# Token sums of the down parts made where each pair is turned, token scales inside the next group, and one early weight chunk split by halves

## The chip, the cores and the metric

The kernel runs on one core of a Trainium2 chip. The metric is the device time of one execution in microseconds (us), the median of several runs. Before the change it is 1868.39 us (three runs, 1868.15 to 1868.74).

## The reference

One layer of a decoder trunk for 256 tokens of width 2048, all in float32. Two token mixers run side by side (a gated recurrent block and stick-breaking attention); their merged output goes through `w_o` and is added to the residual `x`. Then come a SwiGLU feed-forward network and a gated per-layer embedding. The change touches the work from `w_o` on, and the first weights of the kernel:

```python
h = rmsnorm(x, g_mix[i])
proj = h @ w_in[i]                    # starts the kernel: its gate columns come first
...                                   # two mixers
x = x + mix @ w_o[i]

h = rmsnorm(x, g_ffn[i])
gu = h @ w_ffn_gu[i]                  # 2048 -> 2 x 5632
g, u = jnp.split(gu, 2, axis=-1)
x = x + (jax.nn.silu(g) * u) @ w_ffn_down[i]       # 5632 -> 2048

ple_gate = jax.nn.sigmoid(rmsnorm(x, g_ple[i]) @ w_ple_gate[i])
x = x + ple_gate * (p[i] @ w_ple_proj[i])
```

`rmsnorm(x, g)` is `x * rsqrt(mean(x*x) + eps) * g`. The factor `rsqrt(...)` is one number for each token; the kernel multiplies it in after the product ("token scale"), so the product can start before it is known.

## The kernel before

**Products.** Every float32 value is split into a high part `hi` (a rounded copy in the type fp32r) and a low part `lo` (the value less `hi`); a product is three matmuls: `hi*hi`, `hi*lo` of the weights and `lo*hi` of the activations. In function `prod` these are lines 638, 639 and 640: 638 and 639 multiply the high activations by the weights' `whi` and `wlo`, and 640 the low activations by `whi`. The tokens stand on the partitions of the result, 128 tokens by 512 columns for each matmul.

**Weight stream.** The weights come as chunks of 128 rows by 1024 columns in a fixed order. A chunk is loaded by a DMA issued on SP (SyncE), and split by ScalarE (ACT; line 366, `whi`) and then VectorE (DVE; line 367, `wlo`). There are five buffers of each. In the first group the first two k tiles are cut into chunks of 512 columns, so that chunk number 4 is k tile 2, the first of 1024 columns.

**Sums instead of products.** In most groups some k tiles are computed by a Strassen-like scheme of seven products instead of eight. It needs sums of weights and sums of activations. The sums of weights ("11", "T1", "T2", "21", ... and `("S", i, p)`) are made from raw tiles `Q` by DVE adds of 512 or 1024 columns (line 291, function `summed`) and by DMAs that add on landing (line 329, issued on POOL); then they are split like any chunk. The sums of activations are made by `half_sums`: four DVE operations of 128x128, one ACT copy of 512 columns, and one DVE subtraction of 512 columns. They are needed only for the k tiles that take part.

**Groups.** `group` runs the matmuls of one group of output columns over all its slots (a slot is a k tile or a sum). The order from `w_o` on is: wo (2 groups), gu 0 to 3 (each gives 512 feed-forward columns of gate and up), down part dn0 (2 groups), gu 4 to 7, dn1, gu 8 to 10, dn2, and the two groups pg of the per-layer gate. At the end of a group its four PSUM banks are added to the saved tiles by DVE (`tt(c, q, c, ALU.add)`, "ps adds", `H<-ps,H`). Two lists hold work that is put off into the next group: `todo` (for gu the gating, `gated`: a Silu on ACT and a `scalar_tensor_tensor` on DVE at line 449, both with the token scale `rs1`) and `pend` (the turnings: PE transposes of a pair of 128-column blocks, lines 1169 and 1230, after which the pair is split into `hi` and `lo` as the activations of a later product). In each group `TURNED_AT` says at which slots a turning is taken from `pend`.

**The sums of a down part.** The 16, 16 and 12 k tiles of dn0, dn1 and dn2 are pairs of what gu made. Of three, three and two of these pairs the activation sums are wanted. Before the change `parts_sums` makes them late, in the last gu group ahead of the down part (gu 3, 7 and 10), at slots 16, 18 and 20: a DVE add of 512 columns rebuilds the value from `hi` and `lo`, and `half_sums` follows.

**Token scales.** `token_scales` adds up eight partial sums of squares (two small DVE adds) and computes the inverse root by a logarithm and an exponential on ACT. It is called between groups: `rs1` between wo and gu 0, `rs2` between dn2 and pg 0.

**What sets the order.** The engines run their instructions in the order of five lists that a scheduler makes ahead of time from the program. `behind_splits` and `issue_after` tell it not to place an instruction ahead of a given one (the latest split of weights, or a matmul).

Of the kernel before, what the change touches and what calls it, by code (L numbers as in the profile page):

```python
# [8 lines left out]
F32 = mybir.dt.float32  # L9
# [6 lines left out]
D = 2048  # L16
# [28 lines left out]
W_BUFS = 4  # L45
RAW_AHEAD = 12.0
SUMS_AHEAD = 2
TURNED_AT = {True: (5, 7, 9, 11), False: (9, 11, 13, 15)}
NEG = -1e30


# [8 lines left out]
def is_sum(x):  # L60

    return isinstance(x, str) or isinstance(x, tuple) and x[0] == "S"
# [180 lines left out]

DMA_ORDER, DMA_UPTO = dma_order()
HALVES = (1, 3)


class Stream:
# [99 lines left out]
    def split_to(self, n):  # L348
        n = min(n, len(CHUNKS))
        while self.n_split < n:  # L350
            self.sum_to(self.n_split + 1)
            j = self.n_split
            i, a, b = CHUNKS[j]
            mode = PLAN[i][0][3] if PLAN[i][0][0] == "tok" else 0
            if is_sum(mode):
                t, c = self.sums.pop(j)
            else:
                t, c = self.raw.pop(j)[0], P * (b - a)
            o = 512 * (j in HALVES)
            if not o:  # L360
                hi = self.hi = self.phl.tile([P, 1024], F32R, tag="whi", name=f"whi_{j}")
                lo = self.lo = self.phl.tile([P, 1024], F32R, tag="wlo", name=f"wlo_{j}")
            else:
                hi, lo = self.hi, self.lo
            h, l = hi[:, o:o + c], lo[:, o:o + c]
            self.hi_ins = self.nc.scalar.activation(h, t[:, :c], AF.Copy)  # L366
            self.lo_ins = self.nc.vector.tensor_tensor(l, t[:, :c], h.bitcast(F32), ALU.subtract)  # L367
            res = self.parts.setdefault(i, [])
            for x in range(c // P):
                s = slice(o + x * P, o + (x + 1) * P)  # L370
                res.append((hi[:, s], lo[:, s], hi, lo, o + x * P))
            self.n_split += 1
            g = lambda m: (*PLAN[i][0][1:3], m)
            if mode == "T2":
                self.joins(self.raw[g("R")], 0, g("21"), 0)
            elif isinstance(mode, tuple) and mode[:2] == ("S", 2):
                self.joins(self.raw[g(("Y", mode[2]))], 512, g(("S", 1, mode[2])), 512)
# [41 lines left out]
def tile_hybrid_block(ctx: ExitStack, tc: tile.TileContext, xT: bass.AP, x: bass.AP, pT: bass.AP,  # L419
# [25 lines left out]
    def tt(o, a, b, op):  # L445
        nc.vector.tensor_tensor(o, a, b, op)  # L446
# [255 lines left out]
    def group(at, pairs, sums, after=None, also=()):  # L702
# [6 lines left out]
        name, g = at  # L709
        slots = [x for n, y, _, _, _, sl in HEAD + TAIL if (n, y) == at for x in sl  # L710
                 if isinstance(x, int) or is_sum(x)]
        seq = [(n, q, 0, 512) for n, x in enumerate(slots) for q in products(x, pairs_of(name)[:2])]
        if at == LAST_GROUP:
            k = len(slots) - 4
# [11 lines left out]
        for i, (n, (b, y, p, c), e0, e1) in enumerate(seq):  # L726
            if n not in got:
                if n in also:
                    also[n]()
                if n and todo:  # L730
                    todo.pop(0)()
                elif n in TURNED_AT[slots[2] == 6 and slots[8] == "22"] and pend:
                    with tc.issue_after(mm_.ins):
                        pend.pop(0)()
                got[n] = S_.take(("tok", name, g, slots[n]))
# [419 lines left out]

    def token_scales(i, r):
        v = ssq[i]
        tt(v[:, :4], v[:, :4], v[:, 4:], ALU.add)
        tt(v[:, :2], v[:, :2], v[:, 2:4], ALU.add)
        rsqrt_mean(r, v[:, :2], D)  # L1160

    def turned(p):

# [27 lines left out]
    for g in range(2):  # L1191
# [8 lines left out]
            squares(0, t, b)  # L1200
        for p in range(4 * g, 4 * g + 4):
            pend.append(next_h(hg, hsum, p, PC_GF))
    token_scales(0, rs1)


    acts, asum = {}, {}
    behind = {3: 0, 7: 1, 10: 2}

    def gu(g):
        also = {}  # L1210
        if g in behind:
            also = {16 + 2 * i: (lambda p: lambda: parts_sums(acts, asum, p))(p)
                    for i, p in enumerate(pairs_of(f"dn{behind[g]}"))}
        c11, c21, c12, c22 = whole(("gu", g), hg, hsum, also)
        def gated(c, s_, t):
            def run():
                actv(s_, s_, AF.Silu, scale=rs1[:, t:t + 1])
                stt(c, c, rs1[:, t:t + 1], s_, ALU.mult, ALU.mult)
            return run

        todo.extend([gated(c12, c11, 0), gated(c22, c21, 1)])

        def turn(f):
            def run():
                ps = psum()
                for e in range(2):
                    for t, a in enumerate((c12, c22)):
                        c = (2 * f + e) * P
                        o = e * 256 + t * P
                        nc.tensor.transpose(ps[:, o:o + P], a[:, c:c + P], ident)  # L1230
                acts[2 * g + f] = split(ps, "A")
            return run

        pend.extend(turn(f) for f in range(2))
# [14 lines left out]
    for name, g, _, _, _, _ in TAIL:  # L1249
        if name == "gu":  # L1250
            gu(g)
        elif name[:2] == "dn":
            down(int(name[2]), g)
    token_scales(1, rs2)
    pts = [split(pt, "X")]


# [14 lines left out]
        return run  # L1272

    for g in range(2):
        qs_, t_ = group(("pg", g), h3, sum3, also={len(FIRST3) - 4: embedded(g)})
        for n, (q, c) in enumerate(zip(qs_, ("11", "T3", "T2", "T1"))):
            t, b, op = n % 2, 2 * g + n // 2, ALU.add
            c, ps, o = t_[c], pp.pop(0), tl("T")
# [76 lines left out]
```

## Time and profile before

| | us |
|---|---|
| median of three runs | 1868.39 (1868.15 to 1868.74) |
| the profiled execution, its own time | 1867.5 |
| its span in the trace | 1865.5 |
| TensorE matmuls busy in it | 1848.0 (99%) |
| VectorE busy | 1504.6 (81%) |
| ScalarE busy | 1250.0 (67%) |
| GpSimd busy | 115.6 (6%) |

The profiled execution is 0.9 us below the median, and 2.0 us of its time lie outside the span. The mean granted clock of TensorE was 0.999 of full speed. Where groups begin and end in the span: wo to gu 0 at 1059 us, gu 3 to dn0 at 1228, gu 7 to dn1 at 1481, dn2 to pg 0 at 1760.

In the timeline a row has the start in us from the span's beginning, the duration in us, engine, line, operation, the tiles written and read with their shapes, the count of like instructions joined in the row, and in brackets the idle time of the engine just before, with what ended it. PE is TensorE. A wide matmul with 512 columns is followed by the next one after 0.227 us while nothing is waited for, though each row shows 0.39 us, since matmuls overlap. So the time that PE loses at a place is the distance of two starts less 0.227 us; it is up to 0.16 us more than the idle time in brackets. The page's names leave the numbers of buffers out.

### The profile page before, as it was taken

What the parts mean: (1) busy time and instruction counts of PE and PEld (TensorE: products, weight loads), DVE (VectorE), ACT (ScalarE), POOL (GpSimd) and SP (SyncE); (2) the same over time, 40 slices, a digit from 0 to 9 for tenths busy, and PEclk for the clock granted to TensorE, in tenths of its full rate; (3) what the DMA queues carried; (4) which work ended last, traced back from release to release, by engine and by line L of the source; (5) the groups of instructions that cost most, each with busy time, mean ns of one, the idle gap of its engine ahead of it and who ended that gap; (6) DMA issues with size and microseconds to landing.
All of it is one profiled execution on the core that took longest, in us unless ns stands there. A gap on an engine that the chain in (4) does not pass through costs nothing.

```text
span 1865.5 us, 24702 instructions
## 1 busy us (share of the span) xinstructions
PE 1848.0 (99%) x8885; PEld 1551.7 (83%) x8885; DVE 1504.6 (81%) x1896; ACT 1250.0 (67%) x1670; POOL 115.6 (6%) x140
## 2 busy tenths in 40 slices
PE   9999999999999999999999999999999999999998
PEld 7899889888888888888888788878888788888787
DVE  7688887677887576667799888898788988889886
ACT  6587888775566576677666766665566665666774
POOL 0000000000010000000000011100111001110100
PEclk9999999999999999999999999999999999999999
DMA  8556556677786654556788688877888788887774
GB/s 285 182 176 186 191 188 198 205 226 247 249 242 190 190 167 152 165 169 218 229 241 259 211 255 240 250 228 246 260 255 254 219 233 249 250 254 231 205 236 141
DMA packets 121082, 409.11 MB, mean 219 GB/s; under 512 B 13568, under 2 KB 14208, under 8 KB 120960
## 3 DMA queue, kind: packets, MB, share of 16 engines
q1 hardware_dynamic: 101808, 359.82, 55.7%
q0 software_dynamic: 19008, 47.72, 15.5%
q8 instruction: 69, 1.13, 0.2%
q14 instruction: 53, 0.43, 0.1%
q10 hardware_dynamic: 144, 0.01, 0.0%
HBM read 405.40 MB, written 2.10 MB: 218 GB/s over the span
## 4 chain that ended last, share of the span: by engine, by line
PE 94%; DVE 3%; ACT 1%; issue 1%; DMA 0%; SPq 0%; ACTq 0%; DVEq 0%
PE ps L640 25%; PE ps L639 25%; PE ps L638 25%; PE ps L568 9%; PE ps L572 5%; PE ps L552 1%; PE ps L551 1%; PE ps L550 1%; DVE wlo L367 1%; DVE H L446 1%; ACT whi L366 1%; PE ps L1230 1%; DVE Q L291 0%; PE ps L997 0%; DMA w<-in_w_dram 0%
## 5 line engine op out<-in xcount | busy, mean ns | idle before, releaser
L639 PE MATMUL ps<-wlo,Q 128*128 128x512 f32 x2185 | 851.8, 390 | 4.9 <-DVE wlo L367 4.9
L640 PE MATMUL ps<-whi,Q 128*128 128x512 f32 x2185 | 848.7, 389 | 0.0
L638 PE MATMUL ps<-whi,Q 128*128 128x512 f32 x2185 | 774.6, 391 | 5.0 <-ACT whi L366 5.0
L367 DVE TENSOR_TENSOR wlo<-w,whi 128x1024 fp32r<-128x1024 f32 (+2 forms) x497 | 599.6, 1212 | 213.6 <-ACT whi L366 208.7
L366 ACT ACTIVATE whi<-w 128x1024 fp32r<-128x1024 f32 (+2 forms) x497 | 518.7, 1049 | 258.3 <-PE ps L640 200.5
L638 PEld LDWEIGHTS ps<-whi,Q 128*128 128x128 f32 x2185 | 409.1, 188 | 92.8 <-ACT whi L366 10.2
L639 PEld LDWEIGHTS ps<-wlo,Q 128*128 128x128 f32 x2185 | 410.4, 188 | 89.5 <-DVE wlo L367 6.1
L366 ACT ACTIVATE whi<-Q 128x1024 fp32r<-128x1024 f32 (+1 forms) x339 | 339.2, 1006 | 214.0 <-PE ps L640 188.6
L640 PEld LDWEIGHTS ps<-whi,Q 128*128 128x128 f32 x2185 | 410.2, 188 | 84.8 <-DVE Q L446 0.2
L367 DVE TENSOR_TENSOR wlo<-Q,whi 128x1024 fp32r<-128x1024 f32 (+1 forms) x339 | 390.5, 1159 | 67.4 <-ACT whi L366 65.4
L329 POOL DMA_DIRECT2D Q<-in_w_dram x132 | 113.1, 864 | 1701.5 <-DVE Q L291 507.9
L568 PE MATMUL ps<-Q,whi 128*128 128x512 f32 x704 | 170.7, 392 | 0.0
L568 PEld LDWEIGHTS ps<-Q,whi 128*128 128x128 f32 x704 | 128.7, 188 | 24.5
L291 DVE TENSOR_TENSOR Q<-Q,Q 128x512 f32<-128x512 f32 (+1 forms) x132 | 115.7, 890 | 8.6 <-DMA Q<-in_w_dram 8.3
L446 DVE TENSOR_TENSOR H<-H,H 128x512 f32<-128x512 f32 (+1 forms) x208 | 117.0, 574 | 0.9 <-ACT H L452 0.5
L452 ACT ACTIVATE H<-ps 128x512 f32<-128x512 f32 (+1 forms) x163 | 84.6, 534 | 47.2 <-PE ps L640 35.8
L446 DVE TENSOR_TENSOR H<-ps,H 128x512 f32<-128x512 f32 (+1 forms) x154 | 88.7, 606 | 17.6 <-PE ps L640 12.2
L572 PEld LDWEIGHTS ps<-Q,wlo 128*128 128x128 f32 x704 | 90.4, 191 | 3.5
L572 PE MATMUL ps<-Q,wlo 128*128 128x256 f32 x704 | 91.5, 283 | 0.0
L452 ACT ACT_TABLE_LOAD x53 | 68.0, 1283 | 1.7 <-DVE Q L446 0.7
L452 ACT ACTIVATE Q<-H 128x512 fp32r<-128x512 f32 x61 | 37.5, 626 | 40.1 <-DVE H L446 39.7
L446 DVE TENSOR_TENSOR Q<-H,Q 128x512 fp32r<-128x512 f32 (+1 forms) x69 | 47.3, 688 | 1.0 <-ACT Q L452 0.7
(122 smaller groups left out, 905.2 us busy)
## 6 DMA issues: line engine op xcount, KB each, us to landing
w<-in_w_dram SPq DMA_DIRECT2D x473, 512.0 KB, 4.2
Q<-in_w_dram SPq DMA_DIRECT2D x182, 512.0 KB, 5.9
Q<-in_w_dram POOLq DMA_DIRECT2D x50, 512.0 KB, 6.3
Q<-in_w_dram POOLq DMA_DIRECT2D x82, 256.0 KB, 4.9
w<-in_w_dram SPq DMA_DIRECT2D x16, 448.0 KB, 3.3
H<-in_x_dram SPq DMA_DIRECT2D x8, 256.0 KB, 7.3
H<-in_xT_dram SPq DMA_DIRECT2D x7, 256.0 KB, 5.6
out_dram<-H SPq DMA_DIRECT2D x7, 256.0 KB, 2.8
```

Of the source, the lines that this page charges most:

```text
L291: add = lambda o, a, b: self.nc.vector.tensor_tensor(o, a, b, ALU.add)
L329: self.nc.gpsimd.dma_start(t[:, c:], src[:, a:a + 1024 - c], accum_op=ALU.add)
L366: self.hi_ins = self.nc.scalar.activation(h, t[:, :c], AF.Copy)
L367: self.lo_ins = self.nc.vector.tensor_tensor(l, t[:, :c], h.bitcast(F32), ALU.subtract)
L446: nc.vector.tensor_tensor(o, a, b, op)
L452: nc.scalar.activation(o, i, f, **kw)
L550: nc.tensor.matmul(o, wt[0], xh, start=start, stop=False)
L568: nc.tensor.matmul(pss[e], wt[0], rhs(xs, k), start=(k == 0), stop=(k == n - 1))
L572: nc.tensor.matmul(pss[e][:, :256], wt[1], rhs(xs, k)[:, :256], start=False, stop=False)
L638: nc.tensor.matmul(ps, x[0], wh, start=start, stop=False, skip_group_check=goes_on)
L639: nc.tensor.matmul(ps, x[0], wl, start=False, stop=False, skip_group_check=goes_on)
L640: return nc.tensor.matmul(ps, x[1], wh, start=False, stop=stop, skip_group_check=goes_on)
```

## The change

1. Chunk 4 alone is split as two halves of 512 columns (`SPLIT_BY_HALVES`): two ACT copies and two DVE subtractions in place of one each.
2. The activation sums of the down parts' pairs are made where the pair is turned, in the next gu group: pairs 0 and 1 in gu 1, pair 2 in gu 2, 8 and 9 in gu 5, 10 in gu 6, 16 and 17 in gu 9. For these the turned PSUM bank is copied by ACT into an SBUF tile `h`, and the split and `half_sums` read `h`. The DVE add of `parts_sums` falls away (eight times).
3. `token_scales` stands behind the latest splits, and runs at slot 10 of gu 0 (`rs1`) and of pg 0 (`rs2`).
4. In the two groups of dn2, the turnings are taken at slots 6, 8, 10, 12 (before: 9, 11, 13, 15).

The diff (line numbers behind the change are 4 to 7 higher: 366 and 367 become 370 and 371, 291 becomes 292, 446, 449 and 452 become 450, 453 and 456):

```diff
-TURNED_AT = {True: (5, 7, 9, 11), False: (9, 11, 13, 15)}
+TURNED_AT = {"first": (5, 7, 9, 11), "twelve": (6, 8, 10, 12), "even": (9, 11, 13, 15)}
...
+SPLIT_BY_HALVES = (4,)
...
-            self.hi_ins = self.nc.scalar.activation(h, t[:, :c], AF.Copy)
-            self.lo_ins = self.nc.vector.tensor_tensor(l, t[:, :c], h.bitcast(F32), ALU.subtract)
+            w = 512 if j in SPLIT_BY_HALVES else c
+            for e in range(0, c, w):
+                q = slice(e, e + w)
+                self.hi_ins = self.nc.scalar.activation(h[:, q], t[:, q], AF.Copy)
+                self.lo_ins = self.nc.vector.tensor_tensor(l[:, q], t[:, q], h[:, q].bitcast(F32), ALU.subtract)
...
+        turned_at = TURNED_AT["twelve" if len(slots) == len(TWELVE) else
+                              "first" if slots[2] == 6 and slots[8] == "22" else "even"]
...
-                elif n in TURNED_AT[slots[2] == 6 and slots[8] == "22"] and pend:
+                elif n in turned_at and pend:
...
-        tt(v[:, :4], v[:, :4], v[:, 4:], ALU.add)
-        tt(v[:, :2], v[:, :2], v[:, 2:4], ALU.add)
-        rsqrt_mean(r, v[:, :2], D)
+        with behind_splits():
+            tt(v[:, :4], v[:, :4], v[:, 4:], ALU.add)
+            tt(v[:, :2], v[:, :2], v[:, 2:4], ALU.add)
+            rsqrt_mean(r, v[:, :2], D)
...
-    token_scales(0, rs1)
...
-    behind = {3: 0, 7: 1, 10: 2}
+    summed = [p for q in range(3) for p in pairs_of(f"dn{q}")]
...
-        also = {}
-        if g in behind:
-            also = {16 + 2 * i: (lambda p: lambda: parts_sums(acts, asum, p))(p)
-                    for i, p in enumerate(pairs_of(f"dn{behind[g]}"))}
+        also = {10: lambda: token_scales(0, rs1)} if g == 0 else {}
...
-                acts[2 * g + f] = split(ps, "A")
+                p = 2 * g + f
+                if p in summed:
+                    h = tl("T")
+                    actv(h, ps, AF.Copy)
+                    acts[p] = split(h, "A")
+                    asum[p] = half_sums(h)
+                else:
+                    acts[p] = split(ps, "A")
...
-    token_scales(1, rs2)
...
-        qs_, t_ = group(("pg", g), h3, sum3, also={len(FIRST3) - 4: embedded(g)})
+        qs_, t_ = group(("pg", g), h3, sum3, also={len(FIRST3) - 4: embedded(g)} | (
+            {} if g else {10: lambda: token_scales(1, rs2)}))
```

How the order of instructions moves, at three places. In the rows `whi_516` and `wlo_516` are the two parts of chunk 516; `w32`, `Q` are raw weights, `H` working tiles, `ps` PSUM banks; in `Q_738<-H_737` a number names one tile, and the numbers of tiles differ a little between the two kernels.

VectorE around the start of dn0 (chunk 513 is its first, "11", 514 is `("S", 1, 2)`, 515 the k tile 6, 516 is "T1", 517 is `("S", 2, 2)`, 518 the k tile 7), before:

```order
L446 TENSOR_TENSOR Q_733_11115<-H_732_11110,Q_733_11115 128x512
L446 TENSOR_TENSOR H_716_10880<-ps_712_10846,H_716_10880 128x512
L446 TENSOR_TENSOR H_730_11088<-ps_713_10860,H_730_11088 128x512
L291 TENSOR_TENSOR Q_725_11054<-Q_725_11054,Q_734_11118 128x1024
L446 TENSOR_TENSOR H_722_10988<-ps_714_10864,H_722_10988 128x512
L446 TENSOR_TENSOR H_719_10937<-ps_715_10868,H_719_10937 128x512
L446 TENSOR_TENSOR Q_738_11145<-H_737_11140,Q_738_11145 128x512
L291 TENSOR_TENSOR Q_740_11174<-Q_729_11076,Q_735_11129 128x512
L446 TENSOR_TENSOR H_557_8918<-H_557_8918,H_743_11229 128x512
L449 SCALAR_TENSOR_TENSOR H_722_10988<-H_722_10988,rs1_8916,H_716_10880 128x512
L449 SCALAR_TENSOR_TENSOR H_719_10937<-H_719_10937,rs1_8916,H_730_11088 128x512
L367 TENSOR_TENSOR wlo_516_11185<-Q_725_11054,whi_516_11184 128x1024
```

and with the change:

```order
L292 TENSOR_TENSOR Q_734_11086<-Q_734_11086,Q_737_11130 128x1024
L371 TENSOR_TENSOR wlo_515_11173<-w32_515_11084,whi_515_11172 128x1024
L450 TENSOR_TENSOR H_725_10912<-ps_721_10878,H_725_10912 128x512
L450 TENSOR_TENSOR H_736_11110<-ps_722_10892,H_736_11110 128x512
L371 TENSOR_TENSOR wlo_516_11187<-Q_734_11086,whi_516_11186 128x1024
L450 TENSOR_TENSOR H_731_11020<-ps_723_10896,H_731_11020 128x512
L450 TENSOR_TENSOR H_728_10969<-ps_724_10900,H_728_10969 128x512
L371 TENSOR_TENSOR wlo_517_11208<-Q_740_11176,whi_517_11207 128x1024
L292 TENSOR_TENSOR Q_734_11086<-Q_734_11086,Q_742_11220 128x1024
L453 SCALAR_TENSOR_TENSOR H_731_11020<-H_731_11020,rs1_8918,H_725_10912 128x512
L453 SCALAR_TENSOR_TENSOR H_728_10969<-H_728_10969,rs1_8918,H_736_11110 128x512
L371 TENSOR_TENSOR wlo_518_11225<-w32_518_11139,whi_518_11224 128x1024
```

The three L446 rows that make sums of pairs (`Q_733`, `H_737`, `Q_738`) are gone from here; two of the four ps adds and the two gating rows (L449, now L453) stand behind the splits of chunks 516 and 517, where they stood ahead of 516.

ScalarE around the start of gu 0 (chunks 427, 428, 429, 430 are `("S", 2, 2)`, the k tile 7, "T2" and "21" of gu 0), before:

```order
L366 ACTIVATE whi_427_9737<-Q_628_9682 128x1024
L366 ACTIVATE whi_428_9749<-w32_428_9654 128x1024
L452 ACT_TABLE_LOAD
L452 ACTIVATE rs1_8916<-ssq0_8914,eps_t_103 128x2
L452 ACT_TABLE_LOAD
L452 ACTIVATE rs1_8916<-rs1_8916 128x2
L452 ACTIVATE H_643_9802<-ps_642_9784 128x512
L452 ACTIVATE Q_645_9812<-ps_644_9807,prm_sb_76 128x256
L366 ACTIVATE whi_429_9764<-Q_613_9521 128x1024
L366 ACTIVATE whi_430_9785<-Q_630_9700 128x1024
```

and with the change:

```order
L370 ACTIVATE whi_427_9735<-Q_628_9684 128x1024
L370 ACTIVATE whi_428_9747<-w32_428_9656 128x1024
L456 ACTIVATE H_643_9800<-ps_642_9782 128x512
L456 ACTIVATE Q_645_9810<-ps_644_9805,prm_sb_76 128x256
L370 ACTIVATE whi_429_9762<-Q_613_9523 128x1024
L370 ACTIVATE whi_430_9783<-Q_630_9702 128x1024
```

The two table loads and the two small activations that make `rs1` no longer stand between `whi_428` and `whi_429`. They stand behind chunk 439 now, ten slots on:

```order
L370 ACTIVATE whi_439_9951<-w32_439_9831 128x1024
L456 ACT_TABLE_LOAD
L456 ACTIVATE rs1_8918<-ssq0_8916,eps_t_103 128x2
L370 ACTIVATE whi_440_9958<-w32_440_9885 128x1024
L456 ACT_TABLE_LOAD
L456 ACTIVATE rs1_8918<-rs1_8918 128x2
```

ScalarE around the start of pg 0 (chunks 793 to 797 are its "T1", `("S", 2, 2)`, k tile 7, "T2" and "21"), before:

```order
L366 ACTIVATE whi_793_15685<-Q_1025_15498 128x1024
L452 ACTIVATE Q_1047_15676<-ps_1046_15671,prm_sb_76 128x256
L366 ACTIVATE whi_794_15721<-Q_1045_15655 128x1024
L366 ACTIVATE whi_795_15735<-w32_795_15638 128x1024
L452 ACT_TABLE_LOAD
L452 ACTIVATE rs2_8917<-ssq1_8915,eps_t_103 128x2
L452 ACT_TABLE_LOAD
L452 ACTIVATE rs2_8917<-rs2_8917 128x2
L366 ACTIVATE whi_796_15750<-Q_1025_15498 128x1024
L366 ACTIVATE whi_797_15771<-Q_1049_15683 128x1024
```

and with the change:

```order
L370 ACTIVATE whi_793_15687<-Q_1035_15538 128x1024
L370 ACTIVATE whi_794_15719<-Q_1047_15667 128x1024
L370 ACTIVATE whi_795_15733<-w32_795_15650 128x1024
L370 ACTIVATE whi_796_15748<-Q_1035_15538 128x1024
L370 ACTIVATE whi_797_15769<-Q_1049_15685 128x1024
```

Here too the four instructions of `rs2` and a part of the turnings (`Q_1054`, `Q_1047`) are gone from between the splits.

## The prediction

> **What bounds the kernel now.** I read the page first: the span, the busy times, the shares of the chain that ended last, and then the waits of TensorE (columns: us in all, times, longest).
>
> ```profile
> span 1865.5 us, 24702 instructions
> PE 1848.0 (99%) x8885; PEld 1551.7 (83%) x8885; DVE 1504.6 (81%) x1896; ACT 1250.0 (67%) x1670; POOL 115.6 (6%) x140
> PE 94%; DVE 3%; ACT 1%; issue 1%; DMA 0%; SPq 0%; ACTq 0%; DVEq 0%
> ...
> PE ps L638 <- ACT whi L366: 5.0, 10, 1.0
> PE ps L639 <- DVE wlo L367: 4.9, 3, 2.1
> ```
>
> TensorE bounds it, and the change leaves its work as it is. Only what PE waits can be won: ten waits for `whi` and three for `wlo`, 9.9 us of idle time, and a little more in lost spacing, since a wait costs the distance of two starts less 0.227 us. So I went to the timeline at each of these waits. They stand at four places, and the change touches each. I take them in order of time.
>
> **A. The start.** Chunk 4 is the first of 1024 columns. PE (rows 3 and 4) waits for its `wlo`.
>
> ```profile
> 10.73 1.06 ACT L366 ACTIVATE whi<-w 128x1024 fp32r<-128x1024 f32 x1 [0.35 <-DMA w<-in_w_dram]
> 11.82 2.52 DVE L367 TENSOR_TENSOR wlo<-w,whi 128x1024 fp32r<-128x1024 f32 x2 [0.90 <-ACT whi L366]
> 11.90 0.44 PE L638 MATMUL ps<-whi,Q 128*128 128x512 f32 x1
> 13.11 0.50 PE L639 MATMUL ps<-wlo,Q 128*128 128x512 f32 x1 [0.76 <-DVE wlo L367]
> ...
> 8.78 0.63 ACT L366 ACTIVATE whi<-w 128x512 fp32r<-128x512 f32 x1 [1.96 <-DMA w<-in_w_dram]
> 9.44 0.69 DVE L367 TENSOR_TENSOR wlo<-w,whi 128x512 fp32r<-128x512 f32 x1 [1.78 <-ACT whi L366]
> ```
>
> The loss is 13.11 − 11.90 − 0.23 = 0.98. With halves (0.63 and 0.69 from the last two rows), the first `whi` half ends at 10.73 + 0.63 = 11.36 and its `wlo` at about 11.39 + 0.69 = 12.08; PE asks for them at 11.90 and 12.13. The second half is wanted six matmuls after 11.90, at 13.27; it is ready by about 12.7. Two halves take 2 × 0.69 = 1.38 where one piece takes 1.22 to 1.26, so chunk 5 is split about 0.1 later, 14.35 where PE now asks at 14.6. Everything behind is asked for 1.0 earlier. **Term: −1.0**, bounds −1.1 (0.98 and the 0.1 of broken spacing behind) and −0.6 (if the DMA were late by 0.4 again, as the bracket of the first row shows it was 0.35).
>
> The Trainium skill (VectorE: DVE Perf Modes, section on the TRN2 errata) speaks against such halving: an instruction that reads SBUF pays a fixed cost each time, about 150 cycles, which an estimate at 0.96 GHz makes 0.16 us. The rows agree (1.38 against 1.22), and by that rule alone chunk 4 would cost 0.16 more; the wait it removes is six times that.
>
> **B. wo to gu 0.** ACT makes the token scale here, and PE waits for the two splits behind it.
>
> ```profile
> 1066.39 1.28 ACT L452 ACT_TABLE_LOAD   x1
> 1069.40 0.58 ACT L452 ACTIVATE H<-ps 128x512 f32<-128x512 f32 x1
> 1069.88 0.46 ACT L452 ACTIVATE Q<-ps,prm_sb 128x256 fp32r<-128x256 f32 x1
> 1070.23 2.95 ACT L366 ACTIVATE whi<-Q 128x1024 fp32r<-128x1024 f32 x3
> ...
> 1070.43 0.39 PE L640 MATMUL ps<-whi,Q 128*128 128x512 f32 x1
> 1071.35 0.51 PE L638 MATMUL ps<-whi,Q 128*128 128x512 f32 x1 [0.52 <-ACT whi L366]
> 1072.29 0.50 PE L638 MATMUL ps<-whi,Q 128*128 128x512 f32 x1 [0.44 <-ACT whi L366]
> ```
>
> ACT spends 1066.39 to 1069.40, 3.0 us, on the block that moves. Without it the two copies from PSUM run when PE has ended them, 1068.05 to 1068.6 and 1068.95 to 1069.4 (the transposes end at about 1068.98, so this second one cannot go earlier). The three `whi` then start at 1069.3 instead of 1070.23, 0.93 earlier. The first (0.98 apart, 2.95 for three) ends at 1070.35, before PE asks at 1070.66: the first loss, 1071.35 − 1070.43 − 0.23 = 0.69, goes. The second ends at 1071.3 and PE asks at about 1070.85: 0.5 of the second loss (0.72) stays. **Term: −1.1** with 0.2 of broken spacing. Bounds: −0.6 (only the first wait), −1.6 (both and the spacing).
>
> The block itself lands ten slots on, where the splits of weights have 6 to 8 us of lead (from the end of each split's row to the start of the matmul that uses it first), against 3.0 of ACT's time. It is needed by the gating, in gu 1.
>
> The Trainium skill (ScalarE: Activation LUTs, section What ACT_TABLE_LOAD costs) gives 1.28 us for the load and 1.38 for a drain. The load agrees; the drain is not seen, as the two loads and two activations take 3.0 and not 5.3 us. By the page's price B would be the same, since the copies then wait for PE, and the moved block would still fit its cover.
>
> **C. gu 3 to dn0, and gu 7 to dn1.** This is the largest. Rows of DVE, then of PE at the two places, then of ACT:
>
> ```profile
> 1228.79 0.29 DVE L446 TENSOR_TENSOR H<-H,H 128x128 f32<-128x128 f32 x1
> 1228.99 0.69 DVE L446 TENSOR_TENSOR Q<-H,Q 128x512 fp32r<-128x512 f32 x1
> 1229.59 1.28 DVE L446 TENSOR_TENSOR H<-ps,H 128x512 f32<-128x512 f32 x2
> 1230.79 1.22 DVE L291 TENSOR_TENSOR Q<-Q,Q 128x1024 f32<-128x1024 f32 x1
> 1231.92 1.29 DVE L446 TENSOR_TENSOR H<-ps,H 128x512 f32<-128x512 f32 x2
> 1233.12 0.69 DVE L446 TENSOR_TENSOR Q<-H,Q 128x512 fp32r<-128x512 f32 x1
> ...
> 1234.92 1.42 DVE L449 SCALAR_TENSOR_TENSOR H<-H,rs,H 128x512 f32<-128x512 f32 x2
> 1236.24 1.23 DVE L367 TENSOR_TENSOR wlo<-Q,whi 128x1024 fp32r<-128x1024 f32 x1
> ...
> 1235.07 0.39 PE L638 MATMUL ps<-whi,Q 128*128 128x512 f32 x1
> 1237.53 0.50 PE L639 MATMUL ps<-wlo,Q 128*128 128x512 f32 x1 [2.07 <-DVE wlo L367]
> 1239.28 0.73 PE L638 MATMUL ps<-whi,Q 128*128 128x512 f32 x2 [0.31 <-ACT whi L366]
> ...
> 1491.07 0.50 PE L639 MATMUL ps<-wlo,Q 128*128 128x512 f32 x1 [2.07 <-DVE wlo L367]
> ...
> 1233.04 1.05 ACT L366 ACTIVATE whi<-Q 128x1024 fp32r<-128x1024 f32 x1
> 1238.17 1.06 ACT L366 ACTIVATE whi<-Q 128x1024 fp32r<-128x1024 f32 x1 [4.07 <-DVE Q L291]
> ```
>
> PE asks for `wlo` of chunk 516 ("T1") at 1235.30; DVE, dense since 1228.8, starts it at 1236.24. The loss is 1237.53 − 1235.07 − 0.23 = 2.23 there, and 1.2 in the splits and spacing that are late behind it: 3.4. The same at dn1. Two things change in DVE's order, shown with the change: 0.2 + 0.6 + 0.6 = 1.4 of half sums leave, and `wlo` 516 comes right behind two ps adds. A ps add cannot start before the last products of gu 3, about 1228.8. From there: two adds of 0.60 to 1230.1, `wlo` 516 (1.14) to 1231.2, against 1235.3 wanted; two adds and `wlo` 517 to 1233.6, wanted at 1237.8; a weight sum (1.13) and the gating (1.32) to 1236.1, then `wlo` 518 to 1237.2, wanted at 1238.9. The least room is about 1 us at chunk 521, which the order puts earlier on PE. So the whole loss goes, twice: **term −6.9**; bounds −5.0 (2.5 each, if the late splits behind are late still) and −7.0.
>
> **D. dn2 to pg 0.** PE's two waits, ACT ahead of the second, and a row of busy times by stretch.
>
> ```profile
> 1767.79 0.50 PE L638 MATMUL ps<-whi,Q 128*128 128x512 f32 x1 [1.04 <-ACT whi L366]
> 1772.81 0.50 PE L638 MATMUL ps<-whi,Q 128*128 128x512 f32 x1 [0.90 <-ACT whi L366]
> ...
> 1768.71 1.28 ACT L452 ACT_TABLE_LOAD   x1
> 1771.72 2.94 ACT L366 ACTIVATE whi<-Q 128x1024 fp32r<-128x1024 f32 x3
> 1746.00:1770.00 24.00, 22.93 (x105) 18.04 (x104) 24.00 (x43) 19.61 (x34) 1.83 (x3) 1.00 0.65 202
> ```
>
> The last row (columns: stretch, its length, then busy time of PE, PEld, DVE, ACT, POOL) shows DVE without an idle moment for 24 us. Turning pairs three slots earlier moves some of its work ahead of 1746, where 1.7 us were idle, and no more. Following the new order by the same durations, the sum for "T1" comes at 1763.8, `whi` 793 by 1765.0 (no wait), `whi` 794 not before 1767.1, where PE asks at 1766.15: 0.95 stays of 1.7 (the 1.20 of this wait with spacing and a smaller one before). The table block (1768.71 to 1771.7) goes, and with it the loss of 1.06. **Term −1.85**, bounds −1.0 (the block alone) and −2.6.
>
> **What the moved work costs.** Each pair gives the gu group where it is turned one ACT copy of the bank and one of sums (0.58 + 0.63, less what a copy from PSUM took more than one from SBUF, about 1.0), and on DVE four small operations (0.2 each) and 0.6, 1.4. Two pairs are 2.8 of DVE and 2.0 of ACT. Gu 1 from slot 9 on:
>
> ```profile
> 1118.00:1144.00 26.00, 26.00 (x120) 21.53 (x119) 19.42 (x21) 17.30 (x21) 1.73 (x2) 1.00 0.81 270
> ...
> DVE wlo L367 <- ACT whi L366: 6.4, 8, 1.8
> 1386.90 0.69 DVE L367 TENSOR_TENSOR wlo<-Q,whi 128x512 fp32r<-128x512 f32 x1 [1.35 <-ACT whi L366]
> ```
>
> DVE is busy 19.4 of 26 us and waits eight times for ACT, 6.4 in all, and ACT in turn for PE to free a buffer; gu 5 shows the same waits (last row). The splits there are 4.5 to 5.8 us ahead of PE, counted the same way, and the work comes one pair at a time, two slots apart. I take **0**. Without the cover a pair costs 1.4 + 1.0 (bounds 0 to 2.4; 0 to 19 for eight). A gain is excluded, since PE loses nothing in those groups.
>
> The sum: −1.0 − 1.1 − 6.9 − 1.85 = −10.8. The profiled execution took 1867.5, so 1856.7; the median of the runs is 0.9 above it, so **1857.6**.
>
> **Rivals.** (1) *Only the half sums' own time is won at C*: the new place of `wlo` 516 is of no use because a late DMA or a late sum holds its `whi`. For it: ACT stood idle 4.07 before 1238.17, for a sum that DVE made late (the last row at C). Against: `whi` 516 began at 1233.04 (the row above that) and was done before PE asked, and the order has the sum for it earlier still. Then C is about 1.9 each, 3.8: 1860.7. Chance 0.10. (2) *ACT and DVE stay dense at B and D*, where ps adds and turnings give the pace, so that nothing comes of these: −7.9, 1860.5; with a table load in the way of one split besides, about 1862. For it: DVE's 24.00 of 24. Chance 0.12. (3) *Slower: the half sums in gu 1, 2, 5, 6 and 9 take the lead of the splits away*. If their 19 us fell on a path with no room, it would be 1857.6 + 19.2 = 1876.8, a loss; it decides once the lead of 4.5 us is eaten and DVE has no idle time between slots, that is, if the new operations wait for one another (DVE to ACT to DVE) with the queue of splits standing behind them. For it: engines run strictly in order, and the chain is three engine changes long. Against: the rows above. Half of it would give 1867. Chance 0.04 of slower, 0.06 for the half that leaves no difference. That the change does not do what it says is excluded by the order rows.
>
> **How the numbers follow.** My forecast has 0.68. The range holds the forecast's own bounds (terms −0.6 − 0.6 − 5.0 − 1.0 = −7.2 to −12.3, so 1856.1 to 1861.2) and rivals 1 and 2: 1855.0 to 1862.5, leaving out 0.1 to 0.2. A difference of 0.2% (3.7 us) is about what can be told from none, so faster needs a time below 1864.7. All of the forecast and rivals 1 and 2 are there: 0.68 + 0.10 + 0.12 = 0.90, less 0.02 for mishaps; the same 0.07; slower 0.05.
>
> **What would show it.** Right: no wait of PE longer than 0.6 us at the starts of dn0 and dn1, with `wlo` of "T1" over 3 us ahead; 0.98 gone at 11.9; at gu 0 one short wait left for the "21" chunk; at pg 0 one of about 1 us for `("S", 2, 2)` and none for "T2"; PE in gu 1, 2, 5, 6 and 9 without idle time. Wrong: new waits for `wlo` in these gu groups, or a 2 us wait at dn0 that names a `whi`.

## The result, and the profile after

The changed kernel takes 1856.93 us (median of four runs, 1856.49 to 1858.07) beside 1868.27 us for the kernel before. The ratio is 0.9940, with a 95% interval of 0.9923 to 0.9957. The predicted time was 1857.6 us. The profiled execution took 1856.98 us, with a span of 1855.2 us: 10.3 us less span than before, where the prediction's sum was 10.85.

The page of the changed kernel, and the waits of TensorE (us in all, times, longest):

```profile
span 1855.2 us, 24724 instructions
PE 1845.1 (99%) x8885; PEld 1552.7 (84%) x8885; DVE 1499.7 (81%) x1889; ACT 1253.4 (68%) x1679; POOL 115.9 (6%) x140
PE 97%; DVE 1%; DMA 0%; issue 0%; ACT 0%; SPq 0%; ACTq 0%; DVEq 0%
...
PE ps L642 <- ACT whi L370: 2.0, 3, 1.4
...
PE ps L643 <- DVE wlo L371: 0.2, 1, 0.2
```

TensorE's work is the same 8885 matmuls. Its waits for the splits have shrunk from 9.9 us to 2.2, and TensorE now makes up 97% of the chain that ended last. VectorE's 4.9 us less are mostly the eight adds of 0.6 that fell away; ScalarE has the eight copies more.

To see where the time went, I measured the same stretches of the weight stream in both traces: from the first matmul that uses one chunk to the first that uses another. The stretches are wide enough that a matmul or a turning moved within them doesn't count.

| term | stretch (chunks) | before, us | after, us | difference | forecast |
|---|---|---|---|---|---|
| A | span's start to 7 | 21.17 | 19.77 | −1.40 | −1.0 |
| B | 420 to 445, around wo to gu 0 | 55.17 | 54.23 | −0.94 | −1.1 |
| C | 500 to 535, around gu 3 to dn0 | 74.59 | 71.10 | −3.49 | −3.45 |
| C | 634 to 670, around gu 7 to dn1 | 75.91 | 72.43 | −3.48 | −3.45 |
| D | 745 to 812, around dn2 to pg 0 | 141.87 | 140.61 | −1.26 | −1.85 |

The sum is −10.57; 0.3 us came back outside these stretches. At the start of dn0 the timeline of VectorE reads as follows now:

```profile
1224.64 1.22 DVE L292 TENSOR_TENSOR Q<-Q,Q 128x1024 f32<-128x1024 f32 x1
1225.78 1.22 DVE L371 TENSOR_TENSOR wlo<-w,whi 128x1024 fp32r<-128x1024 f32 x1
1226.91 1.28 DVE L450 TENSOR_TENSOR H<-ps,H 128x512 f32<-128x512 f32 x2
1228.11 1.22 DVE L371 TENSOR_TENSOR wlo<-Q,whi 128x1024 fp32r<-128x1024 f32 x1
1229.24 1.28 DVE L450 TENSOR_TENSOR H<-ps,H 128x512 f32<-128x512 f32 x2
1230.44 1.22 DVE L371 TENSOR_TENSOR wlo<-Q,whi 128x1024 fp32r<-128x1024 f32 x1
1231.58 1.22 DVE L292 TENSOR_TENSOR Q<-Q,Q 128x1024 f32<-128x1024 f32 x1
1232.71 1.41 DVE L453 SCALAR_TENSOR_TENSOR H<-H,rs,H 128x512 f32<-128x512 f32 x2
```

The low part of "T1" (chunk 516, fourth row) ends at 1229.33. TensorE uses it first at 1233.01, 3.7 us later; before it waited 2.07 us for it. No wait at all is left at dn0 and dn1.

Besides 0.18 us for chunk 4 at the start, two places still wait. At the start of gu 0 TensorE waits for chunks 427 and 430, as forecast for the second. At the start of pg 0 it waits for the high part of chunk 794, `("S", 2, 2)`. TensorE, and VectorE ahead of that split:

```profile
1758.37 0.50 PE L642 MATMUL ps<-whi,Q 128*128 128x512 f32 x1 [1.44 <-ACT whi L370]
...
1753.76 1.82 DVE L292 TENSOR_TENSOR Q<-Q,Q 128x1024 f32<-128x1024 f32 x2
1755.49 0.48 DVE L453 SCALAR_TENSOR_TENSOR Q<-ps,prm_sb,Q 128x256 fp32r<-128x256 f32 x1
1755.89 0.68 DVE L450 TENSOR_TENSOR Q<-H,Q 128x512 fp32r<-128x512 f32 x1
1756.49 0.68 DVE L292 TENSOR_TENSOR Q<-Q,Q 128x512 f32<-128x512 f32 x1
```

The last row is the second half of the sum for chunk 794. It is ready at 1757.17, its `whi` at 1758.32, and TensorE had asked at 1756.77.

### The profile page after: what moved, and what is told of

Its sections match the earlier page's. It is cut to its first block, busy times and chain, and to the rows that moved or that the text cites. A ratio compares the mean times of both kernels' runs of the same rounds, so it can differ in the third digit from the quotient of the medians.

```text
span 1855.2 us, 24724 instructions
## 1 busy us (share of the span) xinstructions
PE 1845.1 (99%) x8885; PEld 1552.7 (84%) x8885; DVE 1499.7 (81%) x1889; ACT 1253.4 (68%) x1679; POOL 115.9 (6%) x140
## 4 chain that ended last, share of the span: by engine, by line
PE 97%; DVE 1%; DMA 0%; issue 0%; ACT 0%; SPq 0%; ACTq 0%; DVEq 0%
PE ps L643 26%; PE ps L642 26%; PE ps L644 26%; PE ps L572 9%; PE ps L576 5%; PE ps L556 1%; PE ps L555 1%; PE ps L554 1%; DVE H L450 1%; PE ps L1233 1%; DVE wlo L371 0%; PE ps L1003 0%; DMA w<-in_w_dram 0%; PE ps L1176 0%; ACT whi L370 0%
## 5 line engine op out<-in xcount | busy, mean ns | idle before, releaser
L456 ACT ACTIVATE H<-ps 128x512 f32<-128x512 f32 (+1 forms) x171 | 89.4, 537 | 52.6 <-PE ps L644 41.4
L456 ACT ACTIVATE Q<-H 128x512 fp32r<-128x512 f32 x69 | 42.2, 626 | 35.7 <-DVE H L450 35.1
L450 DVE TENSOR_TENSOR Q<-H,Q 128x512 fp32r<-128x512 f32 (+1 forms) x77 | 52.4, 685 | 0.8 <-ACT Q L456 0.7
```

Source lines behind the costliest of these rows:

```text
L456: nc.scalar.activation(o, i, f, **kw)
```

## The experiments

Times are medians, each beside runs of the kernel before on the same chip. Those runs of the kernel before had medians of 1868.02, 1868.1 and 1868.0 us for the three batches.

### One part of the change at a time

Each of these is the kernel before with one hunk of the diff shown above.

**Halves alone** (`SPLIT_BY_HALVES = (4,)` and the loop over halves).

> The kernel before with chunk 4 alone split by halves, nothing else of the change. By the forecast's term A the wait of 0.98 us for the low part of chunk 4 goes and the time falls by 1.0 us, to about 1867.3; in the trace the two low halves end before TensorE asks. Rival: what counts at the start is when the weights land, and the wait only changes its place; then the time stays at 1868.3 within 0.4 us, and the wait for chunk 4 names its high part or is seen on a later chunk.

Measured: 1867.08 us, ratio 0.9994 (0.9985 to 1.0003). By the time alone this can't be told from no change. The trace tells more: TensorE doesn't wait for chunk 4 there (its low halves are two rows in one, its matmul has no bracket).

```profile
10.70 1.29 DVE L371 TENSOR_TENSOR wlo<-w,whi 128x512 fp32r<-128x512 f32 x2 [0.95 <-ACT whi L370]
...
11.15 0.39 PE L642 MATMUL ps<-whi,Q 128*128 128x512 f32 x1
11.45 0.50 PE L643 MATMUL ps<-wlo,Q 128*128 128x512 f32 x1
```

The first matmul on chunk 7 starts at 19.52 us here. In the five profiles of this study without halves (the kernel before, and the runs on scales, sums, turnings and earlier sums alone) it starts at 20.37 to 21.17, mean 20.73; in the nine with halves (this run, the changed kernel and the seven that start from it) at 19.44 to 20.34, mean 19.82. So term A is about 0.9 us on average, and the 1.40 in the pair of traces above holds 0.5 of chance. The wait for chunk 4 itself, in spacing, is 0.56 to 1.01 us in the five (mean 0.81) and 0 to 0.50 in the nine (mean 0.14), so 0.7 of the 0.9 can be put down to it.

**Token scales alone** (`behind_splits`, `rs1` at slot 10 of gu 0, `rs2` at slot 10 of pg 0).

> The kernel before with the token scales alone moved to slot 10 of gu 0 and pg 0. By terms B and D: 0.9 to 1.1 us at the start of gu 0 and 1.0 us at the start of pg 0, so about 1866.2. Rival 2 (ACT and DVE stay dense there, the wait for the next split takes the place of the one removed): less than 0.5 us at each place, 1867.5 to 1868.3.

Measured: 1865.64 us, ratio 0.9987 (0.9978 to 0.9996), 2.4 us under the kernel before. The stretches give 54.23 us for B (all of its 0.94) and 140.61 for D (all of its 1.26). Rival 2 is out for the removed waits: nothing took their place there.

**The sums alone** (made in `turn`, `parts_sums` no longer called).

> The kernel before with the down parts' sums alone made where the pair is turned. By term C the whole loss at the starts of dn0 and dn1 goes, 3.4 us each: about 1861.4, with no loss in gu 1, 2, 5, 6 and 9. Rival 1: only the half sums' own time is won, 1.9 each: about 1864.5. Rival 3: TensorE waits in the gu groups that got the work, and the time is above 1866.

Measured: 1859.93 us, ratio 0.9957 (0.9944 to 0.9969), 8.1 us under the kernel before. The stretch from chunk 500 to 535 is 71.07 us and that from 634 to 670 is 72.43: the whole of C, 3.5 us each, from this part alone. The 8.1 is 1.1 more than C. What that is made of isn't shown: 0.5 of it is that the profiled execution of the kernel before, 1867.5 us, lies under the median of its runs, and for the rest the last section has a candidate.

**The turnings of dn2 alone** (slots 6, 8, 10, 12).

> The kernel before with the turnings of dn2 alone at slots 6, 8, 10, 12. By term D this gives 0.2 to 0.85 us at the start of pg 0 (1867.4 to 1868.1), as only a part of the turned pairs' work finds idle time on DVE earlier. Rival: the two small gains at pg 0 need the token scales out of the way as well, so nothing by itself: 1868.3. Rival on the other side: a wait inside the second group of dn2, up to 1 us slower.

Measured: 1867.36 us, ratio 0.9998 (0.9989 to 1.0007). Stretch D is 141.81 us, 0.06 less than before. The forecast's 0.85 us for this part isn't there. The two waits at pg 0 (0.19 and 1.20 in spacing, worked out from the prediction's rows and those beside them) became one of 1.69. VectorE did do more work ahead of 1746 us: from 1735 on it was busy 7.36 us of 11, where it had been busy 6.29. But the second half of the sum for chunk 794 ends at 1766.65 us in the one trace and at 1766.68 in the other. In the 22 us behind 1746 VectorE was busy 21.46 us, where it had been busy all 22, so half of what was gained there went idle. What else holds the sum to its time wasn't tested.

### Undoing the turnings, and an attempt on the wait that is left at pg 0

From the changed kernel, the turnings of dn2 were put back:

```diff
-TURNED_AT = {..., "twelve": (6, 8, 10, 12), ...}
+TURNED_AT = {..., "twelve": (9, 11, 13, 15), ...}
```

> The changed kernel with the turnings of dn2 back at slots 9, 11, 13, 15. Term D counted 0.85 us for turning earlier; the runs of one part alone spoke against it (alone it made one wait of 1.7 us out of waits of 0.2 and 1.2, and the token scales alone took the other). So by these the time stays or falls by 0.2 us, with two short waits at pg 0, 1.5 us in all with spacing instead of 1.7. By the forecast it would rise by 0.8 us.

Measured: 1856.84 us, where the changed kernel had 1856.93. Stretch D is 140.63 against 140.61. So the fourth part of the change is worth nothing here, neither way.

The other attempt takes work off VectorE in the second group of dn2: the four small operations of each `half_sums` of pg's pairs go to GpSimd (three pairs, twelve instructions).

```diff
-                sums[p] = half_sums(h)
+                sums[p] = half_sums(h, None if hs is hg else nc.gpsimd)
```

> The changed kernel with the four small operations of the half sums of pg's pairs on GpSimd instead of VectorE: 0.8 us less of DVE for each pair, 2.4 us in the second group of dn2 if three pairs are there. If the wait of 1.6 us left at pg 0 comes from DVE being dense, the weight sum of T1 then stands ahead of the ps adds and the wait goes: 1.6 us under the changed kernel. If the wait is set by the ps adds, which can't start before TensorE ends dn2, it stays: no change. Slower by a few us if GpSimd takes so long for 128x128 that the sums themselves are late.

> The same on GpSimd, with the turnings of dn2 at slots 9, 11, 13, 15. By a dense DVE the place of the turnings matters less once 2.4 us are taken off it: within 0.4 us of the run with them early. If the earlier turnings are what makes room for the sums, this is 0.5 to 1.5 us slower than that run.

Measured: 1857.73 us with the early turnings, and 1859.4 with the late ones: 0.8 and 2.5 us slower than the changed kernel. The 0.8 is little beside what single executions differ (1857.53 to 1858.96 us here, 1856.49 to 1858.07 there), but stretch D tells the same: it is 1.1 us longer than in the changed kernel with the early turnings, and 2.6 us with the late ones. The two kernels differ by 1.7 us, so beside sums on GpSimd the place of the turnings matters, and by more than either expectation gave. The timeline of GpSimd and VectorE in the first of these shows two things that bear on it.

```profile
1738.05 2.02 POOL L647 TENSOR_TENSOR H<-H 128x128 f32<-128x128 f32 x2 [2.05 <-ACT H L456]
1740.14 1.65 POOL L647 TENSOR_TENSOR H<-H,H 128x128 f32<-128x128 f32 x2
1741.76 2.31 POOL L647 TENSOR_TENSOR H<-H 128x128 f32<-128x128 f32 x2
...
1743.67 0.95 DVE L450 TENSOR_TENSOR H<-H,H 128x512 f32<-128x512 f32 x1
1745.41 1.48 DVE L371 TENSOR_TENSOR wlo<-w,whi 128x1024 fp32r<-128x1024 f32 x1
1746.82 0.68 DVE L450 TENSOR_TENSOR Q<-H,Q 128x512 fp32r<-128x512 f32 x1
```

One 128x128 operation follows the next after 0.8 to 1.2 us on GpSimd, against some 0.2 on VectorE. And while GpSimd works (to 1745.8), VectorE's own operations are longer: 0.95 instead of 0.68 us, and 1.48 instead of 1.22. So VectorE gained less than the 2.4 us counted. The order of the program did move the sum for "T1" ahead of the ps adds, as expected, but the wait only went over to the low part of that same chunk, 793 (1.45 us). Why the late turnings lose 1.7 us here, and nothing where VectorE makes the sums, wasn't found.

### What C comes from: the place of the split, or the load on VectorE

The forecast named two things: 1.4 us of half sums that leave the boundary, and the new place of the split of "T1" right behind two ps adds. This kernel is the changed one with the low part of that split held back to its old place, behind four ps adds and both gating operations (and the splits behind it with it; `HELD` are the two chunks, `most` stops the splits ahead of them, `gate` is the latest gating operation):

```diff
+                with self.tc.issue_after(self.gate.ins) if j in HELD else nullcontext():
-                self.lo_ins = ...
+                    self.lo_ins = ...
...
-        self.split_to(j + 1 + self.asp)
+        self.split_to(min(j + 1 + self.asp, most))
```

> The changed kernel, but the low part of chunk 516 (and of its like in dn1) is held behind all four ps adds and both gating operations, as it stood before; the half sums stay away. The forecast named two causes for term C, 1.4 us of half sums that leave and the new place of the split. By the durations the split would end at about 1232 where it is wanted at about 1233, so no loss: the time of the changed kernel within 0.4 us, and the new place is worth nothing by itself. If the place is what counts (rival 1 turned round), 1.5 us or more are lost at each of dn0 and dn1: 3 to 4 us over the changed kernel.

Measured: 1856.87 us, the changed kernel's time within 0.1, and no wait at dn0 or dn1. VectorE there:

```profile
1224.82 1.22 DVE L373 TENSOR_TENSOR wlo<-w,whi 128x1024 fp32r<-128x1024 f32 x1
1226.20 2.48 DVE L453 TENSOR_TENSOR H<-ps,H 128x512 f32<-128x512 f32 x4 [0.17 <-PE ps L647]
1228.61 1.48 DVE L456 SCALAR_TENSOR_TENSOR H<-H,rs,H 128x512 f32<-128x512 f32 x2
1230.00 2.36 DVE L373 TENSOR_TENSOR wlo<-Q,whi 128x1024 fp32r<-128x1024 f32 x2
```

VectorE even waits 0.17 us for TensorE to end gu 3, and the split, in its old place, is done at 1231.2, 2.7 us before TensorE uses it. The new place is worth nothing by itself.

The second kernel is the kernel before with its late sums at earlier slots of the same group:

```diff
-            also = {16 + 2 * i: (lambda p: lambda: parts_sums(acts, asum, p))(p)
+            also = {8 + 2 * i: (lambda p: lambda: parts_sums(acts, asum, p))(p)
```

> The kernel before with its late sums (the rebuilding add on DVE included) at slots 8, 10 and 12 of gu 3, 7 and 10 instead of 16, 18 and 20; nothing else. If what costs 3.4 us at dn0 and dn1 is only that the half sums stand in DVE's way between the ps adds and the low part of T1, the whole loss goes here too: by the durations four ps adds, one weight sum and the split end about 2 us ahead of TensorE; about 6.9 us under the kernel before of the same chip. Rival: the form matters (the sums made from the bank when it is turned, the add that falls away), since the same DVE work stays in the same group: no gain at dn0 and dn1, or the splits inside gu 3 become late.

Measured: 1864.86 us, ratio 0.9983 (0.9975 to 0.9992): 3.2 us under the kernel before, not 6.9. TensorE's wait for the low part of "T1" is gone, but one for the next chunk, 517, has come in its place. TensorE, then VectorE:

```profile
1237.52 0.73 PE L638 MATMUL ps<-whi,Q 128*128 128x512 f32 x2 [1.28 <-ACT whi L366]
...
1229.58 2.48 DVE L446 TENSOR_TENSOR H<-ps,H 128x512 f32<-128x512 f32 x4
1231.97 0.68 DVE L291 TENSOR_TENSOR Q<-Q,Q 128x512 f32<-128x512 f32 x1
1232.57 1.22 DVE L367 TENSOR_TENSOR wlo<-Q,whi 128x1024 fp32r<-128x1024 f32 x1
1233.70 1.41 DVE L449 SCALAR_TENSOR_TENSOR H<-H,rs,H 128x512 f32<-128x512 f32 x2
1235.03 0.69 DVE L446 TENSOR_TENSOR H<-H,H 128x512 f32<-128x512 f32 x1
1235.63 1.82 DVE L291 TENSOR_TENSOR Q<-Q,Q 128x512 f32<-128x512 f32 x2
```

The half sums stand far ahead of the boundary here, but the weight sums for chunk 517 (its halves are the second row and the first operation of the last) still come after the ps adds. In the changed kernel both halves are made ahead of the ps adds, which begin at 1226.91:

```profile
1218.89 0.69 DVE L292 TENSOR_TENSOR Q<-Q,Q 128x512 f32<-128x512 f32 x1 [0.67 <-DMA Q<-in_w_dram]
...
1220.63 0.68 DVE L292 TENSOR_TENSOR Q<-Q,Q 128x512 f32<-128x512 f32 x1
```

So most of the 3.5 us isn't due to the half sums' place at the boundary. It is that VectorE came to the end of gu 3 with work left over, and the weight sums were pushed past the ps adds. The load shows it, over the whole group gu 3 (columns: stretch, length, then busy time of PE, PEld, DVE, ACT, POOL), first in this kernel, then in the changed one and in the kernel before:

```profile
1186.00:1228.00 42.00, 42.00 (x191) 34.77 (x190) 40.74 (x56) 27.72 (x34) 4.29 (x5) 1.00 0.86 247
```
```profile
1186.00:1228.00 42.00, 42.00 (x190) 34.71 (x189) 38.50 (x43) 27.84 (x32) 5.82 (x7) 1.00 0.85 236
```
```profile
1186.00:1228.00 42.00, 42.00 (x190) 34.77 (x190) 40.33 (x54) 27.88 (x33) 4.29 (x5) 1.00 0.85 251
```

VectorE has 1.3 us left of 42 in this kernel and 3.5 in the changed one. The kernel before has 1.7 left, but there the last 1.4 us of half sums stand behind the end of the group.

If this is so, a little late work must cost nothing. The third kernel is the changed one with the last pair of each down part (2, 10, 17) made late again, in the old form, at slot 16 of gu 3, 7 and 10:

```diff
-    summed = [p for q in range(3) for p in pairs_of(f"dn{q}")]
+    summed = [p for q in range(3) for p in pairs_of(f"dn{q}")[:-1]]
+    behind = {3: 0, 7: 1, 10: 2}
...
+        if g in behind:
+            also = {16: lambda: parts_sums(acts, asum, pairs_of(f"dn{behind[g]}")[-1])}
```

> The changed kernel with one pair of each down part (2, 10 and 17) made late again, at slot 16 of gu 3, 7 and 10, in the old form; the others where they are turned. If what costs at dn0 and dn1 is that DVE comes to the end of gu 3 and gu 7 with work left over, one pair of three (2.0 of 6.0 us) is caught up before the end, the weight sums for T1 and the next sum stand ahead of the ps adds, and nothing is lost: the time of the changed kernel within 0.4 us. If each late pair costs its own time, a third of the 6.9 us comes back: 2.3 us more.

Measured: 1857.05 us, within 0.2 of the changed kernel; both stretches of C as there (71.07 and 72.43 us). VectorE's load in gu 3 is 38.8 us of 42:

```profile
1186.00:1228.00 42.00, 42.00 (x191) 34.76 (x190) 38.76 (x46) 28.02 (x32) 4.46 (x6) 1.00 0.85 237
```

A third of the moved work, put back, costs none of the 7.0 us: the loss isn't proportional. It is there with 1.3 and 1.7 us left and gone with 3.2 and 3.5 left, which fits a VectorE that can't catch up within the group.

### How much the groups that got the work can take

Both kernels are the changed one, with each of the eight pairs' half sums made over and over into the same tiles. The sums have the same values; only the work is added.

```diff
+        for _ in range(times):          # 3, and 6 in the second kernel
             tt(s1, a21, a22, ALU.subtract)
             ...
             tt(t[:, 512:], q, f32(t[:, :512]), ALU.subtract)
```

> The changed kernel with each of the eight pairs' half sums made three times into the same tiles: per pair 2.8 us of DVE and 1.3 us of ACT more. In gu 1, 5 and 9 DVE would be asked for 22.2 + 5.6 = 27.8 us in 26, 1.8 more than there is, against a lead of the splits of 4.5 us: no loss, the time of the changed kernel within 0.4 us. By rival 3 (the cover was just used up) the 22 us added on DVE show at least by half: 11 us more.

> The same with six times: per pair 7.0 us of DVE and 3.2 us of ACT more. In gu 1, 5 and 9 DVE would be asked for 22.2 + 14 = 36.2 us in 26; less the lead of 4.5 us about 5.7 us are lost in each of these three groups and little in gu 2 and 6: 17 us over the changed kernel, between 8 and 20. If the lead is much larger than read, under 5 us.

Measured: 1865.1 us for three times, 8.2 over the changed kernel where I expected none; 1882.56 us for six times, 25.6 over it where I expected 17, and at most 20. TensorE doesn't wait inside gu 1, 5 and 9, where two pairs each are made, but at the start of the groups behind them. Three times: the waits at the start of gu 6, and VectorE's load in gu 5 and gu 6:

```profile
1407.81 0.73 PE L642 MATMUL ps<-whi,Q 128*128 128x512 f32 x2 [0.31 <-ACT whi L370]
1410.02 1.19 PE L642 MATMUL ps<-whi,Q 128*128 128x512 f32 x4 [1.48 <-ACT whi L370]
...
1356.00:1398.00 42.00, 42.00 (x190) 34.76 (x189) 40.86 (x62) 30.60 (x38) 3.44 (x4) 1.00 0.87 253
1398.00:1439.00 41.00, 39.21 (x175) 31.52 (x173) 40.77 (x59) 28.60 (x36) 5.16 (x6) 1.00 0.80 231
```

VectorE is busy 40.9 us of 42 in gu 5 and 40.8 of 41 in gu 6. The first wait, 0.31, is for the high part of a weight sum (chunk 607); the second is for that of chunk 609, a k tile, which ScalarE splits behind the next weight sum. I had set the added work against the lead of the splits at the slots where it is done, 4.5 us. The lead that counts is the smallest behind it, at the start of the next group. There, in the changed kernel, the high part of chunk 609 is ready 1.6 us ahead of TensorE:

```profile
1403.40 1.05 ACT L370 ACTIVATE whi<-w 128x1024 fp32r<-128x1024 f32 x1
...
1406.08 1.29 PE L642 MATMUL ps<-whi,Q 128*128 128x512 f32 x5
```

The smallest leads at the starts of gu 2, 6 and 10 are 1.6 to 2.3 us. The mechanism of rival 3 is real; the change itself stays inside the cover: in the changed kernel VectorE is busy 39.5 of 42 us in gu 5 and 37.2 of 41 in gu 6, and TensorE loses nothing there.

## Why the prediction was right, and where it wasn't

The forecast was 1857.6 us, and 1856.93 was measured. By its steps:

- **What bounds the kernel** held. All that was won are waits of TensorE for splits, at the four places named.
- **A** (−1.0): held, by the means over the profiles (0.9). In the changed kernel's own trace the 0.18 us for chunk 4 are left, and the wait of 0.96 for an earlier chunk that the forecast left standing isn't there. No run was made for that; it comes and goes with the landing of the first weights.
- **B** (−1.1): held, 0.94, with the rest of the second wait left, as worked out (0.53 in spacing; forecast 0.5). The whole of it comes from the token scales.
- **C** (−6.9): the size held, 6.97, and all of it comes from the sums. Of the two causes given, one fell. "`wlo` 516 comes right behind two ps adds" is not what matters: held in its old place it costs nothing. And "1.4 of half sums leave" is too narrow: moved away from the boundary but kept in gu 3, they still cost 2.1 of 3.5 us at each place. What the runs show in their place is the load on VectorE over the whole group: 6 us of work gone from it for three pairs (0.6 for the rebuilding add and 1.4 for the sums of each), and the weight sums made before the ps adds. Rival 1 is out with it: 3.5 us were won at each place, not 1.9.
- **D** (−1.85): mis-sized. It measured 1.26. The table block was worth 1.26 instead of 1.0, and the term for turning earlier, 0.85, measured nothing in both directions. The step that failed is the tracking of VectorE's new order by hand, which put `whi` 794 at 1767.1 where it is wanted at 1766.15, so 0.95 late; in the trace it came 1.6 late. The idle time ahead of 1746 us was indeed taken, as the forecast had it, but the sum for chunk 794 didn't come earlier by it.
- **The cover of the moved work** (0): held in the result, and no wait is in gu 1, 2, 5, 6 and 9. But the reserve was read from the wrong place, as the runs with repeated sums show. Read from the start of the next group it is 1.6 to 2.3 us, not 4.5. One step of the working is also wrong in its reason: a ScalarE copy of 512 columns takes no longer from PSUM (0.59 us) than from SBUF (0.63). The amount of 2.0 us for two pairs holds all the same: ScalarE's busy time in gu 5 went from 27.62 to 29.63 us, and VectorE's from 36.97 to 39.49, 2.5 where 2.8 was counted.
- The forecast's sum of −10.85 met −10.3 in the span. The medians differ by 11.3; the 1.0 between the two is within what single executions differ, and perhaps holds some of the clock drops below.

## What to carry to other kernels

Find the engine that is late at a boundary, and count its busy time over the whole group ahead of it, not only the operations that stand at the boundary: the loss sets in when it can't catch up, and work that moves to a group with room can be worth more than the part of it that stood at the boundary (3.5 us against 1.4 here). The room in such a group is read from the smallest lead that comes after it, here at the start of the next group (1.6 to 2.3 us), not from the slots where the work is put (4.5). And idle time on an engine is no promise: turning pairs three slots earlier filled some of VectorE's, and brought nothing (0.06 and 0.02 us).

## What the hardware showed beside that

**The clock dropped after a wait of 2 us.** In three of four profiles with the waits of 2.07 us at dn0 and dn1 (halves alone, scales alone, turnings alone, but not the kernel before), one of the two waits was followed by matmuls at half speed. With the token scales alone:

```profile
1236.06 0.69 PE L639 MATMUL ps<-wlo,Q 128*128 128x512 f32 x1 [2.08 <-DVE wlo L367]
1236.54 0.63 PE L640 MATMUL ps<-whi,Q 128*128 128x512 f32 x1
1236.97 0.63 PE L638 MATMUL ps<-whi,Q 128*128 128x512 f32 x1
...
1236.30:1239.30 3.00, 3.00 (x8) 2.29 (x8) 2.95 (x4) 2.60 (x3) 0.00 (x0) 0.50 0.30 53
```

The starts are 0.43 us apart instead of 0.227, and the granted clock of the stretch (the third value from the end) is 0.50. Such a drop made the stretch around the boundary 0.4 to 1.2 us longer than its like without one (75.01 and 75.82 us against 74.59 for dn0, 76.91 against 75.91 for dn1): three of eight such waits had it. None was seen behind the shorter waits at gu 0 and pg 0 in these, but in the kernel with the sums made six times the granted clock falls to 0.50 for 3.3 us or so at three places, each behind a wait of 1.3 to 1.5 us with shorter ones close by. The Trainium skill (TensorE: Matmul & The Clock Gate, section What's actually happening) tells of such a clock gate at half rate, after an idle window of about 3.4 us that runs freely. The half rate, and that it hits only some executions, agrees with the rows; that an idle time of 2.07 us was enough doesn't follow from it. So a wait of this length can cost more than the profile of one execution shows: three drops in eight waits, at 0.4 to 1.2 us, are an estimated 0.3 us for each wait on average. That could be a part of the 1.1 us that the sums alone bring beyond C, but no run shows it: among the executions of the kernel before, those with a listed clock of 0.998 take 1868.0 us on average, and those at 0.999 the same.

**GpSimd slows VectorE.** From start to start, small float32 operations took four to six times as long on GpSimd as on VectorE (0.8 to 1.2 us against 0.20), and beside them VectorE's own took 1.2 to 1.4 times as long (rows above). The Trainium skill (GPSIMD Engine Reference, section 8. Key points) states that the two share their interfaces to SBUF, which agrees, and that VectorE is about twice as fast for such work, which is less than the difference seen here.
